# Strassen's scheme for two groups of each gate/up stage in a two-layer trunk

## The chip, the cores and the metric

The kernel runs on one core of one Trainium2 chip. The metric is the device time of one execution in microseconds (us); less is better.

## The reference

Two layers, each with a half-step SwiGLU, an attention mixer and a second half-step SwiGLU. There are 256 tokens, D_MODEL is 1024 and D_FF is 2816. The change lies in the four SwiGLUs, in the products with w_gate and w_up.

```python
def swiglu(h, w_gate, w_up, w_down):
    return (jax.nn.silu(h @ w_gate) * (h @ w_up)) @ w_down

for i in range(DEPTH):
    h = rmsnorm(x, ffn1_norm[i])
    x = x + 0.5 * swiglu(h, ffn1_w_gate[i], ffn1_w_up[i], ffn1_w_down[i])
    ...                       # projections, self and memory attention, w_out
    h = rmsnorm(x, ffn2_norm[i])
    x = x + 0.5 * swiglu(h, ffn2_w_gate[i], ffn2_w_up[i], ffn2_w_down[i])
```

## The kernel before

Every product of large matrices is made with three TensorE matmuls. Both operands are split into a rounded part (hi) and the rest (lo), and hi\*hi, hi\*lo and lo\*hi are summed in PSUM (`dense`, L409 to L426).

```python
nc.tensor.matmul(out=ps, lhsT=xh, rhs=wh, start=start, stop=False)
nc.tensor.matmul(out=ps, lhsT=xh, rhs=wl, start=False, stop=False)
nc.tensor.matmul(out=ps, lhsT=xl, rhs=wh, start=False, stop=stop)
```

Weights arrive in chunks of 128 x 2048 numbers (1 MB) in `raw` tiles, of which there are three (NRAW). ScalarE rounds a chunk into its `hi` tile, 512 columns at a time (`split_hi`, L321), and VectorE subtracts to get `lo` (`split_lo`, L340). There are four pairs of hi and lo tiles (NHL), called slots here; a slot is free again when the chunk's last matmul is through. So rounding can be up to four chunks ahead of TensorE.

A gate/up stage (`ffn`, L640 to L653) works through 11 groups of 256 gate and 256 up columns. A group needs two chunks (c = 0 and 1, the two halves of the 1024 rows) and both halves of the tokens (tb = 0 and 1). Each chunk is used by 8 calls of `dense`, which are 24 matmuls. `evac` (L517 to L562) takes a finished group out of PSUM: silu on ScalarE (L526), the product and a transpose on VectorE (L529, L537), a store to DRAM (`hd`, L543) and a load back (`hr`, L548), which turns it, then the split of `ht` (L557, L559).

The down stage that follows (L655 to L693) uses chunks of w_down. In three of the four SwiGLUs some chunks (SEVEN) are already done by a seven-product scheme: `split_lo` makes four differences of weights on VectorE (L334), `seven_forms` makes those of h, and `seven_sums` adds the products.

The input of a stage, `Xt`, is made by `prep_half` (L450 to L470): a transposed and scaled tile y, its rounded part xh and the rest xl. Small tiles of 128 x 512 numbers come from a pool of 19 (g2), larger ones from a pool of 12 (g4), and PSUM has 8 banks.

The order of all instructions is fixed while the program is built. `Flow` (L47 to L123) is a planner: it keeps a model clock (0.216 us a matmul, 0.07 + n/960 us on VectorE, 0.15 + n/1200 us on ScalarE, 2.9 us a chunk and 1.5 us latency for a load, 4.0 us from the issue of `hr` to its arrival), and generators add their instructions when the model says that what they wait for is there. Each engine then runs its own instructions in that order. All loads and stores stand in one queue, SP's. Work of `rope_setup` and of the memory's input (`memory_turn`) is mixed into the first stages.

Of the kernel before, what the change touches and what calls it, by code (L numbers as in the profile page):

```python
# [12 lines left out]
F32 = mybir.dt.float32  # L13
# [7 lines left out]
P = 128  # L21
# [121 lines left out]
def kernel(  # L143
# [96 lines left out]
    class Chunk:  # L240
        def __init__(self, parts):
            self.parts = parts
            self.raw = self.hi = self.lo = None
            self.arrive = self.early = None
            self.seven = False
            self.hit = [None] * 7
            self.lot = [None] * 7
            self.tt = [None] * 4
            self.uses = 0

        def part(self, lo, q):
# [13 lines left out]
    def add_chunk(parts, uses=8):  # L265
        c = Chunk(parts)
        c.uses = uses
        c.index = len(chunks)
        chunks.append(c)
        return c  # L270

    def loader():
        for i, c in enumerate(chunks):
# [3 lines left out]
            c.block = lambda q, c=c: c.raw[:, q * 512:(q + 1) * 512] if not c.seven else c.raw[:, (0, 2, 3)[q] * 512:  # L277
                                                                                          (1, 3, 4)[q] * 512]
# [26 lines left out]
    def split_hi():  # L305
        for i, c in enumerate(chunks):
            n = 2 if c.seven else 1
            yield lambda: c.raw is not None and hl_left[0] >= n
            hl_left[0] -= n
            yield c.early or c.arrive  # L310
            c.hi, c.lo = ([whl.tile([P, 2048], F32R, tag=x, name=f"{x}{i}_{j}") for j in range(n)] for x in ("hi", "lo"))
            if not c.seven:
                c.hi, c.lo = c.hi[0], c.lo[0]
            for q in range(7 if c.seven else 4):
                if q == 2:
                    yield c.arrive
                if c.seven and q >= 3:
                    yield lambda: c.tt[q - 3] is not None
                    yield c.tt[q - 3]
                yield calm_a(i)  # L320
                nc.scalar.copy(out=c.part(0, q), in_=c.block(q))  # L321
                c.hit[q] = flow.act(512)

    def split_lo():
        for i, c in enumerate(chunks):
            if c.seven:
                yield lambda: c.hi is not None and g2.left >= 6
                yield c.arrive
                r = [c.raw[:, q * 512:(q + 1) * 512] for q in range(4)]
                t = [g2.take([P, 512], F32, "wsum") for _ in range(4)]  # L330
                c.block = lambda q, r=r, t=t: ([r[0], r[2], r[3]] + t)[q]
                for j, x, y in ((0, r[1], r[0]), (1, r[3], t[0]), (2, r[3], r[1]), (3, r[2], t[1])):
                    yield calm_v(i)
                    nc.vector.tensor_sub(t[j], x, y)  # L334
                    c.tt[j] = flow.dve(512)
            for q in range(7 if c.seven else 4):
                yield lambda: c.hit[q] is not None
                yield c.hit[q]
                yield calm_v(i)
                nc.vector.tensor_sub(c.part(1, q), c.block(q), c.part(0, q).bitcast(F32))  # L340
                c.lot[q] = flow.dve(512)
                if q == 3:
                    raw_left[0] += 1
            if c.seven:
                g2.give(4)
# [16 lines left out]
    SEVEN = {(0, 1): (), (0, 2): (1, 4, 6), (1, 1): (1, 4, 6), (1, 2): (1, 4, 7)}  # L362

# [8 lines left out]

    def plan_ffn(l, nm, wg, wu, wd):
        gu = []
        for g in range(NG):
            ids = []
            for c in range(2):
                pieces = 2 if len(chunks) < 2 else 1
                a = cols4(wg[l], c, g * 256, 256, 0, pieces)
                b = cols4(wu[l], c, g * 256, 256, 256, pieces)  # L380
                ids.append(add_chunk([q for ab in zip(a, b) for q in ab]))
            gu.append(ids)
        plan[l, nm, "gu"] = gu
        dn = []
        for c in range(NG):
            dn.append(add_chunk(turned2(wd[l], c)))
            if c in SEVEN[l, nm]:
                dn[-1].seven, dn[-1].uses = True, 7
        plan[l, nm, "dn"] = dn
# [19 lines left out]
    def dense(ps, xh, xl, ready, c, need, sl, start, stop):  # L409
# [5 lines left out]
        wh, wl = (c.part(0, need), c.part(1, need)) if sl is None else (sl(c.hi), sl(c.lo))  # L415
# [8 lines left out]
        if c.uses == 0:  # L424
            hl_left[0] += 2 if c.seven else 1
# [14 lines left out]
    class Xt:  # L440
        def __init__(self):
# [6 lines left out]
            self.done = [0, 0]  # L448

    def prep_half(xt, tb, hf, gc, wait=0.0):  # L450
# [15 lines left out]
        g2.give()  # L466
# [44 lines left out]
    def ffn(l, nm, xt, gc_next):  # L511
# [5 lines left out]
        def evac(g, ps, end):  # L517
# [3 lines left out]
            for tb in range(2):  # L521
# [11 lines left out]
                banks.give()  # L533
# [15 lines left out]
            yield flow.now + 4.0  # L549
# [41 lines left out]
        def seven(c, ms):  # L591
# [3 lines left out]
            for q, j, m in ((0, 0, 0), (1, 1, None), (2, 6, None), (3, 3, 1), (4, 4, 2), (5, 5, 3), (6, 2, None)):  # L595
                ps = ms[m] if m is not None else acc.ps[q // 6][q // 2 % 2 if q < 6 else 0]
                t = dense(ps, ht[0][:, j], ht[1][:, j], lambda: htt[c], dn[c], q, None,
# [900 lines left out]
```

## Time and profile before

| | us |
|---|---|
| median of 3 runs (964.82 to 967.43) | 965.41 |
| the profiled execution, its own time | 964.95 |
| span of the profiled execution | 963.2 |
| TensorE busy | 954.8 |
| VectorE busy | 745.0 |
| ScalarE busy | 567.9 |

The gate/up stages lie at 9.0 to 130.6, 317.5 to 437.7, 496.9 to 617.1 and 781.2 to 901.4 us of the span; they are called stages 1 to 4 below. TensorE's granted clock is at its upper level from end to end. Busy time of TensorE is modelled and overlaps from one matmul to the next, so distances between starts say more than durations.

### The profile page before, as it was taken

The page shows a single profiled execution, that of the slowest core. Times are in us where ns is not written, and L with a number is a line of the kernel's source. Part 1 is how long each engine was busy: PE and PEld are TensorE (multiplying, and loading weights), DVE is VectorE, ACT ScalarE, POOL GpSimd, SP SyncE. Part 2 cuts the span into 40 slices and gives each one's busy share as a digit, 9 for nine tenths or more (in the row PEclk, how much of TensorE's full clock was granted, in tenths as well). Part 3 has the DMA queues.
Part 4 walks back from the last instruction along what each step waited for, and adds up shares of the span by engine and source line. Part 5 has one row for each costly group of instructions (what it writes and reads, how often), then busy time and mean ns, then how long its engine had stood idle before and what let it go on. Part 6 is the DMA issues. An engine that isn't in the chain of part 4 may idle for free.

```text
span 963.2 us, 13464 instructions
## 1 busy us (share of the span) xinstructions
PE 954.8 (99%) x4525; PEld 783.9 (81%) x4525; DVE 745.0 (77%) x1569; ACT 567.9 (59%) x1215; POOL 60.5 (6%) x65
## 2 busy tenths in 40 slices
PE   8999999999999999999999999999999999999998
PEld 7888888888777888888888888888787788888886
DVE  6777777788777877759986775797989886776785
ACT  6655555666676655545645555565677765554551
POOL 0000000021210000000000000000343100000000
PEclk9999999999999999999999999999999999999999
DMA  8988877486525479766568777666641468777661
GB/s 282 328 267 285 250 263 246 145 272 208 176 88 175 154 224 284 235 229 205 184 208 254 247 245 220 212 202 219 207 143 44 134 196 283 232 254 225 215 190 44
DMA packets 169295, 204.04 MB, mean 212 GB/s; under 512 B 9673, under 2 KB 144394, under 8 KB 169226
## 3 DMA queue, kind: packets, MB, share of 16 engines
q1 hardware_dynamic: 169226, 203.18, 66.0%
q8 instruction: 35, 0.57, 0.2%
q14 instruction: 34, 0.28, 0.1%
HBM read 188.99 MB, written 14.16 MB: 211 GB/s over the span
## 4 chain that ended last, share of the span: by engine, by line
PE 94%; DVE 3%; ACT 1%; DMA 1%; SPq 0%; issue 0%; ACTq 0%
PE gu L422 17%; PE gu L416 17%; PE gu L419 17%; PE acc L416 9%; PE acc L422 9%; PE acc L419 9%; PE pj L422 3%; PE pj L416 3%; PE pj L419 3%; PE xtp L429 1%; PE ptp L429 1%; PE S L1139 1%; PE AV L1220 1%; PE m L422 1%; PE m L419 1%; PE m L416 1%
## 5 line engine op out<-in xcount | busy, mean ns | idle before, releaser
L340 DVE TENSOR_TENSOR lo<-raw,hi 128x512 fp32r<-128x512 f32 x647 | 413.7, 684 | 103.9 <-ACT hi L321 100.0
L321 ACT CAST hi<-raw 128x512 fp32r<-128x512 f32 x647 | 361.7, 618 | 219.0 <-PE gu L422 123.6
L422 PE MATMUL gu<-hi,xl 128*128 128x512 f32 x704 | 274.3, 390 | 0.0
L416 PE MATMUL gu<-hi,xh 128*128 128x512 f32 x704 | 274.1, 389 | 0.0
L419 PE MATMUL gu<-lo,xh 128*128 128x512 f32 x704 | 274.0, 389 | 0.0
L422 PEld LDWEIGHTS gu<-hi,xl 128*128 128x128 f32 x704 | 132.2, 188 | 27.4
L419 PEld LDWEIGHTS gu<-lo,xh 128*128 128x128 f32 x704 | 132.2, 188 | 27.3
L416 PEld LDWEIGHTS gu<-hi,xh 128*128 128x128 f32 x704 | 132.2, 188 | 27.3
L416 PE MATMUL acc<-hi,ht 128*128 128x512 f32 x280 | 109.6, 391 | 0.0
L422 PE MATMUL acc<-hi,ht 128*128 128x512 f32 x280 | 109.2, 390 | 0.0
L419 PE MATMUL acc<-lo,ht 128*128 128x512 f32 x280 | 109.1, 390 | 0.0
L422 PE MATMUL pj<-hi,xl 128*128 128x512 f32 x160 | 64.5, 403 | 0.0
L419 PE MATMUL pj<-lo,xh 128*128 128x512 f32 x160 | 63.6, 397 | 0.0
L416 PE MATMUL pj<-hi,xh 128*128 128x512 f32 x160 | 63.5, 397 | 0.0
L422 PEld LDWEIGHTS acc<-hi,ht 128*128 128x128 f32 x280 | 52.6, 188 | 11.0
L419 PEld LDWEIGHTS acc<-lo,ht 128*128 128x128 f32 x280 | 52.6, 188 | 10.7
L416 PEld LDWEIGHTS acc<-hi,ht 128*128 128x128 f32 x280 | 52.6, 188 | 10.7
L526 ACT ACTIVATE sil<-gu,xr 128x256 f32<-128x256 f32 x88 | 41.5, 472 | 28.6 <-PE gu L422 28.6
L559 DVE TENSOR_TENSOR ht<-hr,ht 128x512 fp32r<-128x512 f32 x35 | 24.1, 687 | 32.2 <-ACT ht L557 32.2
L529 DVE SCALAR_TENSOR_TENSOR h<-gu,xr,sil 128x256 f32<-128x256 f32 x88 | 42.2, 479 | 5.8 <-ACT sil L526 4.5
L557 ACT CAST ht<-hr 128x512 fp32r<-128x512 f32 x35 | 21.6, 618 | 41.9 <-DMA hr<-hd 41.8
L436 POOL TENSOR_TENSOR xr<-v,nhalf 128x1 f32<-128x1 f32 x12 | 8.4, 698 | 502.3 <-DVE v L434 502.3
(191 smaller groups left out, 1069.0 us busy)
## 6 DMA issues: line engine op xcount, KB each, us to landing
raw<-in_ffn_w_down_dram SPq DMA_DIRECT2D x176, 256.0 KB, 4.1
raw<-in_ffn_w_gate_dram SPq DMA_DIRECT2D x86, 512.0 KB, 4.3
raw<-in_ffn_w_up_dram SPq DMA_DIRECT2D x86, 512.0 KB, 5.5
raw<-in_w_in_dram SPq DMA_DIRECT2D x32, 512.0 KB, 4.1
hd<-hb SPq DMA_DIRECT2D x44, 256.0 KB, 2.3
hr<-hd SPq DMA_DIRECT2D x44, 256.0 KB, 5.3
raw<-in_w_out_dram SPq DMA_DIRECT2D x8, 1024.0 KB, 5.0
raw<-in_w_mem_kv_dram SPq DMA_DIRECT2D x4, 1024.0 KB, 5.4
```

Of the source, the lines that this page charges most:

```text
L321: nc.scalar.copy(out=c.part(0, q), in_=c.block(q))
L340: nc.vector.tensor_sub(c.part(1, q), c.block(q), c.part(0, q).bitcast(F32))
L416: nc.tensor.matmul(out=ps, lhsT=xh, rhs=wh, start=start, stop=False)
L419: nc.tensor.matmul(out=ps, lhsT=xh, rhs=wl, start=False, stop=False)
L422: nc.tensor.matmul(out=ps, lhsT=xl, rhs=wh, start=False, stop=stop)
L429: nc.tensor.transpose(out=dst, in_=src, identity=flip if flipped else ident)
L526: nc.scalar.activation(sil, ps[tb][:, 0:256], AF.Silu, scale=xt.r[tb])
L529: nc.vector.scalar_tensor_tensor(out=h, in0=ps[tb][:, 256:512], scalar=xt.r[tb], in1=sil, op0=ALU.mult, op1=ALU.mult)
L557: nc.scalar.copy(out=hi, in_=src)
L559: nc.vector.tensor_sub(lo, src, hi.bitcast(F32))
L1139: nc.tensor.matmul(out=ss[e][:, pr, :nk], lhsT=q[rows, pr, :], rhs=k[rows, pr, :], start=i == 0, stop=i == len(passes) - 1)
L1220: nc.tensor.matmul(out=av[64 * e:64 * e + 64, pr, :], lhsT=vsrc(kb, pr, e), rhs=pts[e][:, pr, kb, :], start=(kb == 0), stop=(kb == nb - 1))
```

## The change

In each of the four gate/up stages two neighbouring groups are taken as a 2 x 2 block matrix times a 2 x 2 block matrix (tokens by rows, rows by groups) and are made with seven block products instead of eight. Groups 2 and 3 are taken in stage 1, and 3 and 4 in the others (PAIR). The four weight chunks r11, r12, r22 and r21 of the two groups give seven items b11, t1, t3, t2, b22, b21 and t4, each used by one block product of 12 matmuls (m1, m5, m7, m6, m3, m2, m4, in this order). t1 to t4 are differences of weights, four VectorE instructions each, before they are split. The items are mixed with the chunks of later groups (p): b11, p, t1, p, t3, p, t2, p, b22, p, p, b21, p, t4. `pair_forms` makes four combinations of y (four VectorE instructions) and splits them (four on each engine); y is kept for that. `pair_sums` copies m1 out of PSUM and adds the products with seven VectorE additions; `evac` then reads the sums from SBUF. A raw tile is held until the last item that reads it is split, and that of a SEVEN chunk until all seven splits are made, where before it was free after the fourth.

Plain chunks of gate/up (all but the first two of the kernel) and b11, b22, b21 are split 1024 columns at a time, t1 to t4 512. The planner takes 6.5 us instead of 4.0 for `hr`. The memory's transposes wait for VectorE a little less strictly, and `memory_prep` waits for all four memory tiles.

```diff
+    class Item:
+        def __init__(self, raws, uses=8, w=1):
...
+            self.n, self.frees, self.takes, self.gives = 1, 1, 0, 0
+            self.sums, self.t = [], []
+            self.index = len(items)
+            w = 1 if len(items) < 2 else w
+            self.units = [(self.own(q, w), q, w, None) for q in range(0, 4, w)]
...
     def split_hi():
+        for i, it in enumerate(items):
+            yield lambda: hl_left[0] >= it.n and all(r.raw is not None for r in it.raws)
...
+            for src, q, w, dep in it.units:
...
+                nc.scalar.copy(out=it.part(0, q, w), in_=src())
+                t = flow.act(512 * w)
...
     def split_lo():
+        for i, it in enumerate(items):
+            if it.sums:
+                yield lambda: all(r.raw is not None for r in it.raws) and g2.left >= it.takes + 2
+                yield max(r.arrive for r in it.raws)
+                it.t += [g2.take([P, 512], F32, "wsum") for _ in range(it.takes)]
+                for j, (x, y) in enumerate(it.sums):
                     yield calm_v(i)
+                    nc.vector.tensor_sub(it.t[j], x(), y())
+                    it.st[j] = flow.dve(512)
+            for src, q, w, dep in it.units:
...
+                nc.vector.tensor_sub(it.part(1, q, w), src(), it.part(0, q, w).bitcast(F32))
...
+            raw_left[0] += it.frees
+            g2.give(it.gives)
...
+    PAIR = {(0, 1): 2, (0, 2): 3, (1, 1): 3, (1, 2): 3}
...
+    def pair_items(raws):
...
+        def m1():
+            made["b11"] = plain(r11, 0)
+        def m5():
+            made["t1"] = sums([r12, r11], 0, 1)
+        def m7():
+            made["t3"] = sums([r22, r12], 0, 1)
+            made["t3"].gives = 4
+        def m6():
+            made["t2"] = sums([r22], 0, made["t1"], made["t1"])
+            made["t2"].frees = 0
+        def m3():
+            made["b22"] = plain(r22, 1)
+        def m2():
+            made["b21"] = plain(r21, 0)
+        def m4():
+            made["t4"] = sums([r21], 0, made["t2"], made["t2"])
+            made["t4"].gives = 4
...
+            for x in ("11", "m1", "p", "12", "m5", "p", "22", "m7", "p", "m6", "p", "m3", "p", "p", "21", "m2", "p", "m4"):
+                work.append(next(p) if x == "p" else x)
...
-            yield flow.now + 4.0
+            yield flow.now + 6.5
...
+        def pair_forms():
+            yield lambda: len(xt.y) == 4 and g4.left >= 4
...
+                yield lambda: flow.free["V"] <= flow.now + SLACK
+                op(y[o], y[a], y[b])
+                flow.dve(512)
+            for j, o in ((0, (1, 1)), (2, (1, 0)), (1, (0, 0)), (3, (0, 1))):
...
+                nc.scalar.copy(out=fm[j][:, 0], in_=y[o])
+                yield flow.act(512)
...
+                nc.vector.tensor_sub(fm[j][:, 1], y[o], fm[j].bitcast(F32)[:, 0])
...
+        def pair_sums():
...
+            nc.scalar.copy(out=u, in_=pb["m1"])
+            yield flow.act(512)
+            banks.give()
+            yield lambda: "m6" in mt and "m7" in mt
+            yield mt["m6"]
+            yield g2.has(3)
+            u2, w, v = (g2.take([P, 512], F32, "gu_v") for _ in range(3))
+            plus(u2, u, pb["m6"])
...
+            plus(w, u2, pb["m5"])
...
+            t = plus(v, w, pb["m7"])
...
+            plus(u2, u2, pb["m7"])
...
+            for m, (g, tb), x in (("m3", (1, 0), w), ("m2", (0, 0), u), ("m4", (0, 1), u2)):
...
+                t = plus(x, x, pb[m])
...
+        def product(m):
...
+            for k in range(4):
...
+                t = dense(pb[m], fh, fl, ready, pit[name], k, k == 0, k == 3)
...
-                yield lambda: flow.free["V"] <= flow.now
+                yield lambda: flow.free["V"] <= flow.now + SLACK
...
-        yield g2.has(8)
+        yield lambda: len(memd) == 4 and g2.left >= 8
```

## Rows read from the trace of the kernel before

**Rows 1.** Page, engines: busy us, share of the span, instructions.
```profile
PE 954.8 (99%) x4525; PEld 783.9 (81%) x4525; DVE 745.0 (77%) x1569; ACT 567.9 (59%) x1215; POOL 60.5 (6%) x65
```
**Rows 2.** Page, the chain that ended last: share of the span by engine.
```profile
PE 94%; DVE 3%; ACT 1%; DMA 1%; SPq 0%; issue 0%; ACTq 0%
```
**Rows 3.** Stretches: stages 1, 2 and 4, and the down stage after stage 3.
```profile
core 0: us, PE busy (x) PEld busy (x) DVE busy (x) ACT busy (x) POOL busy (x), PEclk, DMA share, GB/s
9.00:130.60 121.60, 121.33 (x540) 99.93 (x539) 93.47 (x183) 74.25 (x155) 2.59 (x4) 1.00 0.90 285
317.50:437.70 120.20, 120.20 (x534) 99.52 (x533) 89.48 (x205) 67.24 (x133) 1.81 (x2) 1.00 0.72 228
781.20:901.40 120.20, 120.20 (x534) 99.55 (x533) 85.38 (x164) 67.35 (x133) 1.50 (x2) 1.00 0.72 228
617.10:676.30 59.20, 59.20 (x268) 49.00 (x267) 50.92 (x89) 34.54 (x66) 0.55 (x1) 1.00 0.63 204
```
**Rows 4.** Timeline of PE (start, length, instruction), 78 matmuls in a row, ends shown.
```profile
39.75 0.39 PE L416 MATMUL gu<-hi,xh 128*128 128x512 f32 x1
...
57.20 0.39 PE L422 MATMUL gu<-hi,xl 128*128 128x512 f32 x1
```
**Rows 5.** Timeline of DVE: six in a row, and a difference that reads the one before.
```profile
48.18 3.76 DVE L340 TENSOR_TENSOR lo<-raw,hi 128x512 fp32r<-128x512 f32 x6
...
625.82 0.69 DVE L334 TENSOR_TENSOR wsum<-raw 128x512 f32<-128x512 f32 x1
626.54 0.69 DVE L334 TENSOR_TENSOR wsum<-raw,wsum 128x512 f32<-128x512 f32 x1
```
**Rows 6.** Groups by shape (busy us, mean ns): DVE subtractions of 512 and 256 columns.
```profile
L586 DVE TENSOR_TENSOR h<-sf,h 128x512 fp32r<-128x512 f32 x9 | 6.2, 686 | 0.3
...
L586 DVE TENSOR_TENSOR h<-hr,h 128x256 fp32r<-128x256 f32 x9 | 3.6, 395 | 0.0
```
**Rows 7.** Waits: who waited for whom: us in total, times, longest us.
```profile
ACT hi L321 <- PE gu L422: 123.6, 65, 2.9
DVE lo L340 <- ACT hi L321: 100.0, 85, 2.8
ACT ht L557 <- DMA hr<-hd: 41.8, 25, 2.8
```
**Rows 8.** Timelines of ACT and DVE in stage 2, a chunk split in full lead.
```profile
410.67 2.19 ACT L321 CAST hi<-raw 128x512 fp32r<-128x512 f32 x4 [2.85 <-PE gu L422]
...
411.32 2.50 DVE L340 TENSOR_TENSOR lo<-raw,hi 128x512 fp32r<-128x512 f32 x4 [2.18 <-ACT hi L321]
```
**Rows 9.** Timelines of DVE and PE, stage 4: fourth chunk's last lo, its first matmul.
```profile
790.61 4.29 DVE L340 TENSOR_TENSOR lo<-raw,hi 128x512 fp32r<-128x512 f32 x7
...
798.00 0.39 PE L416 MATMUL gu<-hi,xh 128*128 128x512 f32 x1
```
**Rows 10.** Timelines in stage 1: third chunk's last lo, its first matmul, waits for weights.
```profile
20.20 0.71 DVE L340 TENSOR_TENSOR lo<-raw,hi 128x512 fp32r<-128x512 f32 x1
...
21.39 0.39 PE L416 MATMUL gu<-hi,xh 128*128 128x512 f32 x1
...
24.85 2.18 ACT L321 CAST hi<-raw 128x512 fp32r<-128x512 f32 x4 [1.88 <-DMA raw<-in_ffn_w_up_dram]
...
38.63 2.18 ACT L321 CAST hi<-raw 128x512 fp32r<-128x512 f32 x4 [0.39 <-DMA raw<-in_ffn_w_up_dram]
```
**Rows 11.** Timeline of DVE, a down stage: idle before these two, none between them.
```profile
630.33 0.69 DVE L559 TENSOR_TENSOR ht<-hr,ht 128x512 fp32r<-128x512 f32 x1 [1.29 <-ACT ht L557]
...
649.24 2.50 DVE L340 TENSOR_TENSOR lo<-raw,hi 128x512 fp32r<-128x512 f32 x4 [0.73 <-ACT hi L321]
```
**Rows 12.** Page, DMA issues: count, KB each, median us to landing.
```profile
raw<-in_ffn_w_up_dram SPq DMA_DIRECT2D x86, 512.0 KB, 5.5
...
hr<-hd SPq DMA_DIRECT2D x44, 256.0 KB, 5.3
```

More of the change, by code (lines that the diff above doesn't have):

```diff
@@ L305, in split_hi @@
     def split_hi():
[L306 to L314, printed above, removed]
+        for i, it in enumerate(items):
+            yield lambda: hl_left[0] >= it.n and all(r.raw is not None for r in it.raws)
+            hl_left[0] -= it.n
+            yield max(r.early or r.arrive for r in it.raws)
+            it.hi, it.lo = ([whl.tile([P, 2048], F32R, tag=x, name=f"{x}{i}_{j}") for j in range(it.n)]
+                            for x in ("hi", "lo"))
+            for src, q, w, dep in it.units:
@@ L371, with seven_item @@
     WO = (0, 1, 2, 3)
-    def plan_ffn(l, nm, wg, wu, wd):
[L374 to L382, printed above, removed]
+    def seven_item(it):
+        r = [it.own(q) for q in range(4)]
+        t = lambda j: lambda: it.t[j]
+        it.n, it.uses, it.takes, it.gives = 2, 7, 4, 4
+        it.sums = [(r[1], r[0]), (r[3], t(0)), (r[3], r[1]), (r[2], t(1))]
+        it.units = [(r[0], 0, 1, None), (r[2], 1, 1, None), (r[3], 2, 1, None)] + [(t(j), 3 + j, 1, j) for j in range(4)]
@@ new lines, in pair_items, with sums, plain @@
+    def pair_items(raws):
+        r11, r12, r22, r21 = raws
+        def sums(need, x, y, held=None):
+            it = Item(need, 4)
+            it.t, it.takes = (held.t, 0) if held else ([], 4)
+            at_ = lambda v, j: it.own(j, 1, v) if isinstance(v, int) else (lambda: v.t[j])
+            it.sums = [(at_(x, j), at_(y, j)) for j in range(4)]
+            it.units = [((lambda j=j: it.t[j]), j, 1, j) for j in range(4)]
+            return it
+        def plain(r, frees):
+            it = Item([r], 4, 2)
+            it.frees = frees
+            return it
+        made = {}
+        def m1():
[15 more added lines that the diff above has]
+            made["t4"].gives = 4
+        return made, dict(m1=m1, m5=m5, m7=m7, m6=m6, m3=m3, m2=m2, m4=m4)
@@ L383, in plan_ffn @@
         plan[l, nm, "gu"] = gu
+        plan[l, nm, "work"] = [w for w in work if w not in ("11", "12", "22", "21")]
+        if pair is not None:
+            plan[l, nm, "pair"] = made
         dn = []
@@ L515, in ffn, with evac @@
         prog = [-1]
-        def evac(g, ps, end):
+        def evac(g, ps, end, gives=None):
             hb = None
@@ L654, in ffn @@
+        if pair is not None:
+            flow.spawn(pair_forms())
+        work = list(plan[l, nm, "work"])
+        if (l, nm) != (0, 1):
+            for tb in range(2):
+                for c in range(2):
+                    plain_chunk(0, c, (tb,))
+            work = work[2:]
+        for w in work:
+            if isinstance(w, str):
+                product(w)
+            else:
+                plain_chunk(*w, range(2))
         flow.until(banks.has(4))
         acc = Acc()
-        nxt = None if gc_next is None else Xt()
+        nxt = None if gc_next is None else Xt(nm == 2 and PAIR[l + 1, 1] is not None)
```

198 lines of the change are left out of this document (128 added, 70 removed).

## The prediction

> **What bounds the kernel now.** I read the page's engine table first: TensorE is busy 99% of the span [rows 1], and the chain that ended last is 94% TensorE [rows 2]. Since its busy time is modelled, I then looked at starts. In stage 1 the first matmul of a run of 78 starts at 39.75 us and the last at 57.20 [rows 4], so 17.45 / 77 = 0.2266 us a matmul, with no hole. A stage has 528 of these, 119.7 us, and the stretches of stages 2 and 4 are 120.2 us long [rows 3], a few transposes included: the gate/up stages are bound by TensorE's stream from end to end. Every matmul taken out is worth 0.2266 us, as long as weights stay split ahead of it. So the second thing to read is how far ahead they are, and how much VectorE, which must do most of the new work, has left.
>
> The waits show it. ScalarE's roundings wait most for TensorE's last use of a slot (123.6 us), and VectorE's subtractions for those roundings (100.0 us) [rows 7]: both sit idle because all four slots are full. In stage 2 ScalarE is let go at 410.67, and VectorE has the chunk split at 411.32 + 2.50 = 413.82 [rows 8]. TensorE has just begun the first of the three chunks in front, 3 x 24 x 0.2266 = 16.3 us of work. The full lead is thus 410.5 + 16.3 - 413.8 = 13.0 us. VectorE is busy 85.4 us of stage 4, 89.5 of stage 2, and 93.5 of stage 1 [rows 3].
>
> **The change part by part.** *Matmuls.* Eight block products become seven, 96 matmuls become 84, in four stages: 48 x 0.2266 = 10.9 us off TensorE's stream. Shapes stay, so I expect the same distance. The Trainium skill (TensorE: Matmul & The Clock Gate, section on the back-to-back issue gap) gives about 216 ns for 512 columns; by that the 48 would be worth an estimated 10.4 us. The row shows 0.2266, and the row decides.
>
> *VectorE.* Six subtractions in a row take 3.76 us, the single one 0.686 [rows 5, 6]: a distance of (3.76 - 0.69) / 5 = 0.615 us. Per stage there are new: 16 differences of weights, 12 more splits (28 quarters for 16), 8 instructions for the combinations of y, 7 additions; 43 x 0.615 = 26.4 us. The wide split saves little. A 1024-column subtraction isn't in the trace; from 256 to 512 columns it grows by 0.686 - 0.395 = 0.291 us [rows 6], so I take 0.615 + 2 x 0.291 = 1.197 for 1.230, 0.03 saved, 42 times, 1.4 us (bounds: nothing, and the 0.615 of one whole instruction each). VectorE then has 85.4 + 26.4 - 1.4 = 110.4 us in a stage of 120.2 - 2.7 = 117.5, and 118.5 of 118.9 in stage 1. It fits, barely, so the order in time matters.
>
> *The lead in stages 2 to 4.* I follow it item by item: lead of the next = lead + TensorE's time for this item - VectorE's time for the next. TensorE: 5.44 for a plain chunk, 2.72 for a block product. VectorE: 85.4 / 22 = 3.9 for a plain chunk with all that belongs to it, 8 x 0.615 = 4.9 for t1 to t4, 2.5 for b11, b22, b21. The lowest start is stage 4, where the fourth chunk's last lo ends at 790.61 + 0.69 and is wanted at 798.00 [rows 9]: 6.7 us. The combinations of y fall just there: 6.7 - 4.9 = 1.8. Two plain chunks give back 1.5 each, b11 3.0: 7.8 at b11. Then p 6.6, t1 7.1, p 6.0, t3 6.5, p 5.3, t2 5.8, p 4.6, and four sums fall due (2.5): b22 5.1, p 3.9, and with one group's `evac` (4 x 1.4 us for two groups, so 2.8) and a sum p 2.0, b21 5.0, p 3.8, t4 3.7, p 2.5, and after the last evac about 0.7. From there it grows by 1.5 a chunk. It stays above nothing; I add 0.4 us for the three stages together, with 0 and 2 as bounds. VectorE can hold such a pace: in the down stage after stage 3 it works without a gap from 630.33 to its wait before 649.24, 18 us, [rows 11] with nothing lost on TensorE there.
>
> *Loads.* r11, r12 and r22 are held while they are shared, and three raw tiles are all there are. r22 can only be loaded when t1 is split. A load takes 5.5 us at the median [rows 12], then come four differences, one rounding and four subtractions, some 11.2 us from t1 to t3, where TensorE takes 2.72 + 5.44 = 8.2. That costs 3 us of lead once and caps t3 at 7.1 - 3.0 = 4.1, about 2.4 below the row above; VectorE makes this wait good with other work, so I keep the sum and count it in the bounds. In SP's queue that load waits ahead of `hd` and `hr`, which the down stage needs only after the remaining chunks, five of them at the least (27 us).
>
> *Stage 1.* Here the lead isn't there yet. The third chunk's last lo ends at 20.20 + 0.71 = 20.91 and its chunk is wanted at 21.39; ScalarE still waits for weights at 24.85 and at 38.63 [rows 10]. The last quarter is used 3 x 0.68 = 2.0 us after the first, so the slack is 2.5 us; the combinations of y take 4.9 about then: 2.4 us stall, unless they fall into a wait for weights. Later the shared items take some 7 us of lead (7.8 to 0.7 above) from the 3 to 5 there can be by then: 2 to 4 more. Stage 1 pays between 0 and 7 us; I take 3.5.
>
> *At nothing.* The later rounding of h ends waits of ScalarE for `hr` (41.8 us, 25 times [rows 7]; 5.3 us to land [rows 12] where the planner took 4.0). No matmul waited behind them, so it gains nothing now, but it keeps ScalarE free where the lead is thin; an `hr` tile is held 2.5 us longer. ScalarE gets some 17 instructions more, and has 67 of 120 us [rows 3]. In the down stages a raw tile of a SEVEN chunk comes free three subtractions, 1.8 us, later; three raws in turn and the lead hide that. The memory's input may come later, since it wants nine free small tiles while the new items hold up to eight; its products stand behind the first down stage, whose 61 us I count as its cover.
>
> **The sum.** -10.9 + 3.5 + 0.4 = -7.0 us of the span of 963.2 us: 956.2, with the 1.75 us around it 957.95 for the profiled execution, which lay 0.46 under the median. On the median: 965.41 - 7.0 = 958.4.
>
> **The rivals.** *The cover holds everywhere.* No stall in stage 1 either: 965.4 - 10.9 = 954.5. For it: VectorE has little queued behind the startup's loads, and the sum was made with leads to the last quarter. Against: stage 1's weights still land late at 38 us.
>
> *Stage 1 pays in full, the others 0.5 to 1 each.* 965.4 - 10.9 + 7 + 1.5 to 3 = 963.0 to 964.5. For it: 118.5 of 118.9 us there.
>
> *VectorE can't hold 0.615 (slower).* The leads above end 0.7 us above nothing after some 105 subtraction-lengths (64 us / 0.615). Each 0.01 us more per instruction takes 1.05 us of lead per stage: the stall begins at 0.622, and at 0.65 the three stages lose 3 x 3.0 us, which with stage 1 is all of the gain; that is the point from which it decides. At the full 0.686 they lose 3 x 6.8 = 20 us: 965.4 - 10.9 + 3.5 + 20 = 978. For it: a difference that reads the one before it starts 0.72 us after it [rows 5], and the additions of `pair_sums` are such a chain. Against: these are few, and plain runs hold 0.615. The Trainium skill speaks for this rival (VectorE: DVE Perf Modes, "The DRAIN you can't avoid"): an instruction doesn't start until the pipeline has emptied, which would make the duration the cost. The trace disagrees for a run of subtractions, 0.615 apart where one lasts 0.686.
>
> *It doesn't do what it says*: fewer matmuls, but further apart, by the many short accumulations: 84 instead of 96 only pays below 0.2266 x 96 / 84 = 0.259 us. No row speaks for it.
>
> **How the numbers follow.** A measurement here can tell about 0.3%, 2.9 us, from no change, so faster means below 962.5. Forecast (956 to 961) 0.45; cover everywhere (954 to 956) 0.25; stage 1 in full (961 to 965) 0.20, of which 0.12 below 962.5; slower by VectorE's pace 0.07; the last 0.03, near no change. Faster 0.82, the same 0.11, slower 0.07. The range runs from 954.0 to 963.5: it takes in the cover, and most of the third case, and leaves out less than 2 in 10.
>
> **What would show it.** 4477 matmuls instead of 4525, 0.2266 us apart in m1 to m7. Stages 2 to 4 117.2 to 118.5 us long, stage 1 121 to 125. Holes between starts in stage 1 at the second to fourth chunk and from m7 on, put down to lo (L340's successor), and few elsewhere. ScalarE's wait for slots well under 123.6 us, VectorE near 90% in these stages. The forecast is wrong if holes stand before m7, m6 or m4 in stages 2 to 4, or if the wide splits take far from 1.2 us of VectorE, or if the memory's products come late at the end of the first down stage.

## The result, and the profile after

The changed kernel takes 968.37 us (median of 13 runs, 967.03 to 971.44), the kernel before 965.28 beside it (13 runs): ratio 1.0029, interval 1.0017 to 1.0041. I had forecast 958.4. The times of either kernel differ by up to 5 us from run to run; the profiled execution of after took 970.04 with a span of 968.2, so the accounts below, made of spans, start from 968.2 - 963.2 = +5.0 us, where the medians are 3.1 apart.

First the page of after (engines: busy, share, instructions; then the chain that ended last), which answers [rows 1, 2]:

```profile
PE 951.2 (98%) x4477; PEld 775.1 (80%) x4477; DVE 828.5 (86%) x1577; ACT 586.3 (61%) x1119; POOL 61.9 (6%) x65
...
PE 65%; DVE 17%; DMA 11%; ACT 3%; issue 2%; SPq 1%; POOL 0%; DVEq 0%; ACTq 0%; POOLq 0%
```

The 48 matmuls are gone, but the chain, 94% TensorE before, is 65% TensorE now and runs through VectorE (17%) and DMA (11%). Something that was covered is not covered any more. The table by stretch says where: stages 1 to 4, and fifth the down stage after stage 3, against [rows 3].

```profile
core 0: us, PE busy (x) PEld busy (x) DVE busy (x) ACT busy (x) POOL busy (x), PEclk, DMA share, GB/s
9.00:140.60 131.60, 125.44 (x529) 99.00 (x528) 109.88 (x176) 76.59 (x129) 3.86 (x4) 0.97 0.78 251
328.40:446.00 117.60, 117.60 (x522) 97.43 (x521) 106.93 (x175) 72.02 (x110) 2.54 (x2) 1.00 0.73 230
505.20:622.70 117.50, 117.50 (x522) 97.34 (x521) 105.91 (x173) 70.65 (x108) 0.86 (x1) 1.00 0.75 240
788.50:906.40 117.90, 117.87 (x522) 97.30 (x521) 106.15 (x167) 71.21 (x111) 1.50 (x2) 1.00 0.72 229
622.70:683.60 60.90, 59.70 (x268) 48.75 (x268) 53.12 (x102) 35.61 (x70) 0.55 (x1) 1.00 0.62 203
```

Counted from the first matmul of a stage to the first of the next one, stages 2, 3 and 4 are 2.7, 2.7 and 2.4 us shorter, about what 12 matmuls each were to give. Stage 1 ends 10.05 us later than before, at 140.66 instead of 130.61. The down stage after stage 3 is 1.8 us longer, the first mixer 1.1. Sum: 10.05 + 1.8 + 1.1 - 7.9 = +5.0. So the question is stage 1: it takes 131.5 us where 12 matmuls fewer should leave 121.6 - 2.7 = 118.9. It lost 12.6 us.

Part of that is the clock. Timeline of PE in stage 1, holes (the bracket is the idle time and what ended it; a hole is counted below as the distance between two starts less the usual 0.227 us, a little more than the bracket), and under it stretches of after: one ahead of the holes, and two that follow some of them.

```profile
44.41 0.51 PE L496 MATMUL gu<-hi,xh 128*128 128x512 f32 x1 [0.81 <-ACT hi L326]
45.67 0.51 PE L499 MATMUL gu<-lo,xh 128*128 128x512 f32 x1 [0.76 <-DVE lo L344]
...
69.91 0.50 PE L499 MATMUL gu<-lo,xh 128*128 128x512 f32 x1 [2.12 <-DVE lo L344]
```
```profile
39.70:43.20 3.50, 3.50 (x17) 2.89 (x16) 0.92 (x2) 0.11 (x1) 0.00 (x0) 1.00 0.79 277
46.70:50.10 3.40, 3.40 (x9) 2.66 (x8) 0.50 (x2) 0.00 (x0) 0.00 (x0) 0.50 0.86 270
70.80:73.70 2.90, 2.90 (x8) 2.31 (x7) 2.90 (x4) 0.00 (x0) 0.00 (x0) 0.50 0.91 256
```

After the holes at 43.2 and 44.4 us, and again after the one at 67.4, TensorE ran at its lower level, 1.2 GHz (0.50), for about 3 us: the same matmuls start 0.427 us apart there instead of 0.227, so seven or so cost 1.4 us more each time. The eight longest holes are 7.3 us together, the two slow stretches 2.8. The clock alone doesn't make after the slower kernel: two of its 13 runs have a mean granted clock of 1.000, and they took 967.36 and 968.37 us.

What did stage 1 wait for? The waits of SyncE (SP in the rows), which issues the loads, from 9 to 130 us (us in total, times, longest), first in the kernel before, then after:

```profile
SPq L281 <- DVE lo L340: 21.2, 17, 3.5
SPq L548 <- DMA hd<-hb: 3.0, 3, 1.7
```
```profile
SPq L288 <- DVE lo L344: 32.7, 13, 4.2
SPq L632 <- DMA hd<-hb: 20.0, 6, 5.1
```

The second line has grown from 3.0 to 20.0 us. Timelines of SP and of DVE about the first holes show what it does (start, length, instruction):

```profile
38.35 0.42 SPq L627 DMA_DIRECT2D hd<-hb  x1
43.92 0.37 SPq L632 DMA_DIRECT2D hr<-hd  x1
44.38 0.62 SPq L288 DMA_DIRECT2D raw<-in_ffn_w_gate_dram  x1
45.05 0.46 SPq L288 DMA_DIRECT2D raw<-in_ffn_w_up_dram  x1
45.56 0.46 SPq L288 DMA_DIRECT2D raw<-in_ffn_w_gate_dram  x1
```
```profile
44.39 2.36 DVE L344 TENSOR_TENSOR lo<-raw,hi 128x1024 fp32r<-128x1024 f32 x2 [3.77 <-ACT hi L326]
...
49.65 2.69 DVE L338 TENSOR_TENSOR wsum<-raw,raw 128x512 f32<-128x512 f32 x4 [2.90 <-DMA raw<-in_ffn_w_up_dram]
```

`hr` reads from DRAM what `hd` writes there, so SyncE stands at `hr` until `hd` has landed, 5.5 us. The weight loads stand behind it, though VectorE has nothing to do (idle 3.77 and 2.90 us in these rows). The kernel before had the same two DMAs, but mostly with a weight load between them, issued while `hd` was under way:

```profile
38.50 0.34 SPq L543 DMA_DIRECT2D hd<-hb  x1
39.67 0.37 SPq L281 DMA_DIRECT2D raw<-in_ffn_w_gate_dram  x1
...
42.12 0.37 SPq L548 DMA_DIRECT2D hr<-hd  x1
```

In after no load stands between the first three such pairs. It seemed to me that the raw tiles held for the pair of groups leave none to put there; that wasn't shown, and run e10 (below) speaks against it.

### The profile page after: what moved, and what is told of

Its sections match the earlier page's. It is cut to its first block, busy times and chain, and to the rows that moved or that the text cites. A ratio compares the mean times of both kernels' runs of the same rounds, so it can differ in the third digit from the quotient of the medians.

```text
span 968.2 us, 13306 instructions
## 1 busy us (share of the span) xinstructions
PE 951.2 (98%) x4477; PEld 775.1 (80%) x4477; DVE 828.5 (86%) x1577; ACT 586.3 (61%) x1119; POOL 61.9 (6%) x65
## 4 chain that ended last, share of the span: by engine, by line
PE 65%; DVE 17%; DMA 11%; ACT 3%; issue 2%; SPq 1%; POOL 0%; DVEq 0%; ACTq 0%; POOLq 0%
PE gu L499 9%; PE gu L502 9%; PE gu L496 8%; PE acc L496 7%; DVE lo L344 7%; PE acc L499 7%; PE acc L502 7%; DMA raw<-in_ffn_w_up_dram 4%; PE pj L502 2%; DMA hd<-hb 2%; ACT hi L326 2%; PE pj L499 2%; PE pj L496 2%; DVE wsum L338 2%; DMA raw<-in_ffn_w_down_dram 2%
## 5 line engine op out<-in xcount | busy, mean ns | idle before, releaser
L326 ACT CAST hi<-raw 128x512 fp32r<-128x512 f32 (+1 forms) x467 | 335.5, 769 | 160.0 <-DMA raw<-in_ffn_w_up_dram 53.1
L344 DVE TENSOR_TENSOR lo<-raw,hi 128x512 fp32r<-128x512 f32 (+1 forms) x467 | 390.3, 871 | 31.6 <-ACT hi L326 31.3
L499 PE MATMUL gu<-lo,xh 128*128 128x512 f32 x576 | 226.5, 393 | 4.3 <-DVE lo L344 4.1
L496 PE MATMUL gu<-hi,xh 128*128 128x512 f32 x576 | 226.0, 392 | 0.8 <-ACT hi L326 0.8
L502 PE MATMUL gu<-hi,xl 128*128 128x512 f32 x576 | 225.8, 392 | 0.0
L499 PEld LDWEIGHTS gu<-lo,xh 128*128 128x128 f32 x576 | 108.9, 189 | 30.3 <-DVE lo L344 7.8
L496 PEld LDWEIGHTS gu<-hi,xh 128*128 128x128 f32 x576 | 109.0, 189 | 24.1 <-ACT hi L326 1.2
L502 PEld LDWEIGHTS gu<-hi,xl 128*128 128x128 f32 x576 | 108.9, 189 | 22.3
L326 ACT CAST hi<-wsum 128x512 fp32r<-128x512 f32 x100 | 58.5, 619 | 24.3 <-DVE wsum L338 21.5
L344 DVE TENSOR_TENSOR lo<-wsum,hi 128x512 fp32r<-128x512 f32 x100 | 63.1, 682 | 0.0
L641 ACT CAST ht<-hr 128x512 fp32r<-128x512 f32 x35 | 21.6, 618 | 49.3 <-DMA hr<-hd 49.3
```

What stands on the lines that cost most here:

```text
L326: nc.scalar.copy(out=it.part(0, q, w), in_=src())
L344: nc.vector.tensor_sub(it.part(1, q, w), src(), it.part(0, q, w).bitcast(F32))
L641: nc.scalar.copy(out=hi, in_=src)
```

## The experiments

My theory when I began them: stage 1's loss is `hr` on SyncE's queue. The rivals: three raw tiles are too few while the pair holds them; VectorE can't keep up from a cold start; the memory's transfers crowd the weights. Stage 1 is taken from its first matmul to the first of the down stage, in the profiled execution; "pair" is the first of the two groups in stage 1. Such a length is of one execution: the first matmul comes at 8.8 to 11.6 us, and in e2, e4, e7, e11 and e12 the stage begins with 2 to 5 us at the lower clock, so a difference of a microsecond or two between two lengths says little. The medians are of all runs.

| run | pair | `hd`, `hr` on | raw tiles | median us | ratio (95%) | stage 1 us |
|---|---|---|---|---|---|---|
| before | none | SyncE | 3 | 965.3 | | 121.6 |
| after | 2 | SyncE | 3 | 968.37 | 1.0029 (1.0017 to 1.0041) | 131.5 |
| e1 | none | SyncE | 3 | 960.36 | 0.9946 (0.9930 to 0.9963) | 121.7 |
| e5 | 2 | GpSimd | 3 | 961.64 | 0.9963 (0.9949 to 0.9977) | 125.8 |
| e2 | 4 | SyncE | 3 | 962.21 | 0.9969 (0.9959 to 0.9979) | 126.8 |
| e10 | 2 | SyncE | 4 | 970.60 | 1.0053 (1.0033 to 1.0074) | 130.7 |
| e11 | 2 | GpSimd | 4 | 967.28 | 1.0016 (1.0005 to 1.0027) | 125.4 |
| e12 | 4 | GpSimd | 4 | 962.73 | 0.9976 (0.9966 to 0.9986) | 120.8 |
| e13 | 2, no differences | GpSimd | 4 | 961.98 | 0.9966 (0.9954 to 0.9978) | 119.0 |
| e9 | none | GpSimd | 3 | 958.19 | 0.9928 (0.9908 to 0.9948) | 121.3 |
| e14 | 4 | GpSimd | 3 | 958.66 | 0.9937 (0.9918 to 0.9957) | 120.3 |
| e15 | 4 | GpSimd | 4 | 955.58 | 0.9900 (0.9883 to 0.9916) | 119.3 |

**Is it stage 1?** One run without its pair.

```diff
-    PAIR = {(0, 1): 2, (0, 2): 3, (1, 1): 3, (1, 2): 3}
+    PAIR = {(0, 1): None, (0, 2): 3, (1, 1): 3, (1, 2): 3}
```

> Stage 1 without its pair (all 528 matmuls), stages 2 to 4 as in the changed kernel. If stage 1 is all of the loss and the others keep their 2.7 us each: stage 1 back at 121.4 to 122 us, total 957 to 959 us. If the wide split or the later h are what hurts stage 1, it stays above 125 us and the total above 962.

960.36 us, 8.0 less than after, with stage 1 at 121.7 us as before. SyncE's wait for `hd` up to 130 us is 7.8 us here instead of 20.0, so most of it comes with the pair. The scheme is worth its price where a lead exists; in stage 1 alone it cost all that the others saved and more.

**Is it the queue?** `hd` and `hr` go to GpSimd's queue; the other engines keep their order of instructions to the last one.

```diff
-            nc.sync.dma_start(out=hd.rearrange("a i b x -> (a i) (b x)"), in_=hb.rearrange("p b t f j -> p (b t f j)"))
+            nc.gpsimd.dma_start(out=hd.rearrange("a i b x -> (a i) (b x)"), in_=hb.rearrange("p b t f j -> p (b t f j)"))
...
-            nc.sync.dma_start(out=hr, in_=hd.rearrange("a i b x -> (i b) a x"))
+            nc.gpsimd.dma_start(out=hr, in_=hd.rearrange("a i b x -> (i b) a x"))
```

> Store and load of h issued from GpSimd's queue instead of SP's; the instructions of TensorE, VectorE and ScalarE are the same in the same order. SP's queue theory: weights are loaded as soon as a raw tile is free, stage 1 falls from 131.5 to 122 to 126 us, total 959 to 963. Cold start or VectorE's load: stage 1 stays within 2 us of 131.5 us, total 966 to 970.

Stage 1 falls from 131.5 to 125.8 us; about 2.8 us of the difference are the two slow stretches, which e5, at the upper clock all through stage 1, doesn't have. The timeline of SP for the same stretch of the same program:

```profile
36.95 0.37 SPq L288 DMA_DIRECT2D raw<-in_ffn_w_gate_dram  x1
37.36 0.50 SPq L288 DMA_DIRECT2D raw<-in_ffn_w_up_dram  x1
37.90 0.48 SPq L288 DMA_DIRECT2D raw<-in_ffn_w_gate_dram  x1
38.43 0.50 SPq L288 DMA_DIRECT2D raw<-in_ffn_w_up_dram  x1
```

These two chunks are asked for at 36.95 and 37.90; in after they are the ones of 44.38 and 45.56. This run also settles the two small losses elsewhere: the down stage after stage 3 is back at 59.25 us and from the last matmul of the first down stage to stage 2 it takes 125.9 us, as before. In that down stage after had shown the same picture, four weight loads, `hd`, and 4.6 us later `hr` ahead of the next loads, and some 30 us on TensorE waiting for lo:

```profile
629.16 2.53 SPq L288 DMA_DIRECT2D raw<-in_ffn_w_down_dram  x4
631.73 0.58 SPq L627 DMA_DIRECT2D hd<-hb  x1
636.37 0.36 SPq L632 DMA_DIRECT2D hr<-hd  x1
636.84 22.30 SPq L288 DMA_DIRECT2D raw<-in_ffn_w_down_dram  x20
```
```profile
669.48 0.50 PE L499 MATMUL acc<-lo,ht 128*128 128x512 f32 x1 [0.84 <-DVE lo L344]
```

So of the spans' difference the queue is 968.2 - 959.7 = 8.5 us: 5.7 in stage 1, 1.8 in that down stage, and 1.1 in the first mixer. On the medians it is 6.7.

The same wait can also be shortened by issuing `hr` later, when `hd` is nearer to its end:

```diff
             g2.give()
+            yield flow.now + 4.0
             yield g2.has()
             hr = g2.take([P, 4, P], F32, "hr")
```

> The planner puts the load of hr 7 us after its store instead of 3, so the store has landed and SP doesn't stand still before the weights behind it. SP's queue theory: SP's wait for hd in stage 1 falls from 21.0 us to under 5, stage 1 from 131.5 us to 123 to 127, total 960 to 964. Cold start alone: stage 1 stays within 2 us of 131.5, total 966 to 970.

962.87 us (ratio 0.9973, 0.9963 to 0.9983). SyncE's wait for `hd` from 9 to 140 us falls from 21.0 to 3.1, that for VectorE's lo rises to 51.7, and stage 1 is still 128.3 us long, 1.3 more than I had expected at most. It takes the wait of the queue away and leaves the rest, which I still had to find.

**Is it the memory's transfers?** They go to GpSimd's queue too.

```diff
-        nc.sync.dma_start(out=d.rearrange("a i b x -> (a i) (b x)"), in_=src.rearrange("p b t k j -> p (b t k j)"))
+        nc.gpsimd.dma_start(out=d.rearrange("a i b x -> (a i) (b x)"), in_=src.rearrange("p b t k j -> p (b t k j)"))
...
-        nc.sync.dma_start(out=r.rearrange("p a t k j -> p a (t k j)"), in_=d.rearrange("a i b x -> (i b) a x"))
+        nc.gpsimd.dma_start(out=r.rearrange("p a t k j -> p a (t k j)"), in_=d.rearrange("a i b x -> (i b) a x"))
...
-            nc.sync.dma_start(out=m, in_=mem[0, :, q * 256:(q + 1) * 256].rearrange("(b p) d -> p b d", p=P))
+            nc.gpsimd.dma_start(out=m, in_=mem[0, :, q * 256:(q + 1) * 256].rearrange("(b p) d -> p b d", p=P))
```

> As e5_h_on_pool, and the memory's loads and stores from GpSimd's queue too, so SP issues nothing but weights, gains and x. With h alone moved, stage 1 was 125.8 us and SP still stood 10.2 us before the memory's store. SP's queue theory: stage 1 falls to 120 to 123 us, total 957 to 960. VectorE's load in stage 1, or the raw tiles held at a cold start: stage 1 stays at 125 us or more, total 961 or more.

963.36 us (0.9976, 0.9964 to 0.9989), no better than e5; stage 1 is 124.9 us, and the mixer behind it 1.8 longer. I had expected 120 to 123: the memory isn't the cause.

**Is it the place?** The pair two groups later, when there has been more time to build a lead; on SyncE's queue, and then with the edits of e6.

```diff
-    PAIR = {(0, 1): 2, (0, 2): 3, (1, 1): 3, (1, 2): 3}
+    PAIR = {(0, 1): 4, (0, 2): 3, (1, 1): 3, (1, 2): 3}
```

> Stage 1's pair on groups 4 and 5 instead of 2 and 3, after eight plain chunks instead of four. Cold start (the pair comes before the lead is built): stage 1 falls to 119 to 121 us, total 955 to 957. VectorE's total in stage 1 too high (118 of 119 us), wherever the pair stands: stage 1 stays at 125 us or more, total 961 or more. SP's queue (the load of h waits for its store, weights behind it): in between, since a lead of 12 us covers one such wait.

962.21 us, stage 1 126.8. Now there is one hole, of 4.4 us at 114.8, and its cause stands in SP's timeline:

```profile
108.68 0.45 SPq L627 DMA_DIRECT2D hd<-hb  x1
116.34 0.36 SPq L632 DMA_DIRECT2D hr<-hd  x1
116.76 0.50 SPq L288 DMA_DIRECT2D raw<-in_ffn_w_gate_dram  x1
```

It is the queue again, 7.1 us of waiting for `hd`. What the later place saves, 4.7 us, should then be the other cause.

> Stage 1's pair on groups 4 and 5, and h and the memory on GpSimd's queue; TensorE, VectorE and ScalarE run the same instructions in the same order as in e2_first_at_4, where stage 1 took 126.8 us with one hole of 4.4 us. SP's queue theory: stage 1 at 119 to 121 us, total 954 to 957, the 10.9 us of the 48 matmuls in full. VectorE's load (118 of 119 us) as the cause: stage 1 stays at 124 us or more, total 960 or more.

960.70 us (0.9943, 0.9923 to 0.9963), and 127.6 us for stage 1: by what I had written, both speak for VectorE's load and against the queue. The profile is of its slowest run, 967.26, where stage 1 begins with some 5 us at the lower clock and has a hole of 2.2 us, for lo, at 117.9, so the length says little; but the best runs, 957.8 to 958.6, lie above the 954 to 957 that I had expected too. The expectation failed, and the run leaves open why; e14 below is the same without the memory's transfers.

**What do the other parts of the change do?** All gate/up weights split 512 columns at a time; and h rounded as early as before.

```diff
-            it = Item([r], 4, 2)
+            it = Item([r], 4, 1)
...
-                gu[w] = add_chunk(parts(*w), 8, 2)
+                gu[w] = add_chunk(parts(*w), 8, 1)
```

> All weights of gate/up split 512 columns at a time again, everything else as in the changed kernel. If the wide split helps by its saving (42 times 0.03 to 0.08 us a stage), VectorE has 1.5 to 3.5 us more in each stage, and stage 1 gets up to 4 us longer: total 968 to 973. If it hurts, because the first quarter comes later where the lead is thin: 963 to 967.

973.04 us (1.0067, 1.0048 to 1.0085). Stages 2 to 4 are as short as in after (117.4 each), but stage 1 is 137.4 us. So the wide split, which I had put at 1.4 us of VectorE's time, is worth 5.9 us there (4.7 on the medians) and nothing where a lead is. That points to the work of splitting in stage 1; VectorE's part and ScalarE's, whose roundings get cheaper too (last section), aren't told apart by this run.

```diff
-            yield flow.now + 6.5
+            yield flow.now + 4.0
```

> The planner takes 4.0 us for hr again, everything else as in the changed kernel. The plan is another one after that, so a few us either way say little. If the later rounding costs nothing and gains nothing: within 2 us of 968.4. If the earlier rounding lets ScalarE stand before h while weights wait: ScalarE's wait for hr in stage 1 goes from 6 to over 10 us, total 970 to 974. If the later rounding is itself the harm, 962 to 965.

975.14 us (1.0095, 1.0077 to 1.0114), stage 1 135.3 us, and the down stage after stage 2 is 2.9 longer. ScalarE's wait for `hr` is 94.0 us over the kernel instead of 49.3. I had put the later rounding down at nothing; with leads this thin it is worth 6.8 us, with the other plan that comes with it.

**Is it the number of raw tiles?** A fourth one, paid for with two of the twelve large slots; on SyncE's queue (e10), with the edit of e5 (e11), and with the pair at 4 too (e12).

```diff
-    NRAW, NHL, NT2 = 3, 4, 19
+    NRAW, NHL, NT2 = 4, 4, 19
...
-    gp = ctx.enter_context(tc.tile_pool(name="gp", bufs=12))
+    gp = ctx.enter_context(tc.tile_pool(name="gp", bufs=10))
...
-    g4 = Slots(flow, gp, "g", 12)
+    g4 = Slots(flow, gp, "g", 10)
```

> A fourth raw tile, paid for with two of the twelve four-KB slots; the pair stays at groups 2 and 3 and hd and hr stay on SyncE. Theory (the part of stage 1's loss that GpSimd's queue did not cure, about 6 us, is that three raw tiles are held by the pair, so that weights wait for VectorE's release): stage 1 falls from 131.5 to 124 to 127, and SyncE's wait for lo in it falls well under 33 us. Rival A (only the wait of hr matters, and it delays the fourth tile's load as well): 130 to 132. Rival B (VectorE's own work in stage 1 is the bound): 130 to 132 with VectorE busy without gaps where the holes are. Fewer four-KB slots may cost the down stages 0 to 3 us.

> A fourth raw tile, and hd and hr on GpSimd's queue. Theory (queue and raw tiles are the two causes): stage 1 is 119 to 121.5 us, which is the 119 that seven products in place of eight leave and at most 2.5 of the start, and the time is 955 to 958. Rival (something else, VectorE's pace or the memory, holds stage 1): it stays at 124 to 126, as it was with the queue alone changed (125.8).

Stage 1 is 130.7 us (after: 131.5) and 125.4 (e5: 125.8). My theory of the held raw tiles falls: at this place a fourth tile gives next to nothing on either queue. Nor does it fill the gap between `hd` and `hr`; SyncE's wait for `hd` in e10 is longer than the 20.0 us of after:

```profile
SPq L632 <- DMA hd<-hb: 26.4, 8, 5.0
```

The totals are worse than without it, since the memory's products after the first down stage take 6 to 7 us more (in e11 28.6 for 22.0). But e11 shows what it is instead. Stretches 20 to 60 and 60 to 100 us (columns as above):

```profile
20.00:60.00 40.00, 39.81 (x176) 32.40 (x175) 39.90 (x64) 26.72 (x41) 5.48 (x8) 1.00 0.84 261
60.00:100.00 40.00, 36.80 (x157) 28.57 (x156) 35.19 (x57) 23.96 (x43) 4.41 (x7) 1.00 0.72 232
```

VectorE is busy 39.90 of the 40 us up to 60: it waits for nothing, weights included, and gains no lead. TensorE's large holes come after it, from 72 on, the longest (2.1 us) at 91.8, where VectorE stood 2.04 us at the subtraction for `ht`, with t4's four splits behind it:

```profile
90.31 0.45 DVE L621 STREAM_TRANSPOSE hb<-h 128x256 f32<-128x256 f32 x1
92.80 0.69 DVE L643 TENSOR_TENSOR ht<-hr,ht 128x512 fp32r<-128x512 f32 x1 [2.04 <-ACT ht L641]
93.41 2.49 DVE L344 TENSOR_TENSOR lo<-wsum,hi 128x512 fp32r<-128x512 f32 x4
```

With a lead such a wait is covered; without one it is a hole.

> As the run with four raw tiles and hd and hr on GpSimd's queue, with the pair of stage 1 at groups 4 and 5. Theory (queue and raw tiles are the causes; the place matters little once they are gone): stage 1 119 to 121 us, within 1.5 us of the run with the pair at 2, time 954 to 957.5. Rival (the start is the cause: the place decides): over 2 us shorter than with the pair at 2.

Stage 1 is 120.8 us, 4.6 less than e11 (as the medians are), which differs in the place alone: the expectation's rival, that the place decides.

**Is it VectorE's work?** e11 once more, with the sixteen differences of stage 1 left out (the plan is still empty only there); the blocks are split as they are, so what stage 1 computes for these groups isn't the product. With them go the small tiles that held them, and the wait of a split for its difference.

```diff
             it = Item(need, 4)
             it.t, it.takes = (held.t, 0) if held else ([], 4)
             at_ = lambda v, j: it.own(j, 1, v) if isinstance(v, int) else (lambda: v.t[j])
+            if not plan:
+                it.takes = 0
+                it.units = [(it.own(j), j, 1, None) for j in range(4)]
+                return it
...
-            made["t3"].gives = 4
+            made["t3"].gives = 4 if plan else 0
...
-            made["t4"].gives = 4
+            made["t4"].gives = 4 if plan else 0
```

> The run with four raw tiles and hd and hr on GpSimd's queue, pair at groups 2 and 3; in stage 1 the sixteen differences of weights (t1 to t4) are left out, and the blocks are split as they are, so that what stage 1 computes there is not the product; 16 x 0.615 = 9.8 us of VectorE's work are gone and nothing else of the loads, the matmuls or the queues. Theory (what holds stage 1 once the queue is mended is VectorE, which had no idle time from 20 to 61 us and so built up no lead before the pair's work came): stage 1 falls from 125.4 to 119.5 to 122, and the holes at 91 to 99 us go. Rival (weights or the wait for hr on VectorE's queue hold it): 124 or more.

```profile
20.00:60.00 40.00, 39.81 (x176) 32.51 (x175) 35.30 (x51) 28.22 (x46) 5.24 (x8) 1.00 0.95 301
60.00:100.00 40.00, 40.00 (x178) 32.83 (x177) 35.68 (x58) 25.87 (x43) 4.47 (x7) 1.00 0.86 275
```

Stage 1 is 119.0 us, its holes of over half a microsecond are gone, and VectorE is busy 35.30 of the 40 us. 9.8 us of VectorE's work gave back 6.4 us of stage 1, and 5.3 on the medians. The second cause is the work itself, at a time when there is no lead to pay for it.

**Putting it together.** No pair in stage 1, `hd` and `hr` on GpSimd's queue (e1's and e5's edits); the pair at 4 and the queue (e2's and e5's); and the same with a fourth raw tile, this time for four of the nineteen small tiles.

> No pair in stage 1, and hd and hr on GpSimd's queue. Theory: both causes of the loss are gone; stage 1 is like the one of before, 121 to 122 us, stages 2 to 4 stay at 117.2 to 117.7, the holes in the down stages are absent, and the time is 955 to 958. Rival (the late issue on GpSimd costs elsewhere, as it made ht late before): the time is 959 to 962, no better than the run without the first pair alone (960.4).

> Three raw tiles, hd and hr on GpSimd's queue, pair of stage 1 at groups 4 and 5. Theory (queue and place are two causes that add up: the queue was worth 5.7 us at place 2, the place 4.7 on either queue): stage 1 is 126.8 - 5.7 = 121 (120 to 122) us, time 955 to 958. Rival (the fourth raw tile is what mended it at place 4): stage 1 124 or more, time 959 to 962.

```diff
-    NRAW, NHL, NT2 = 3, 4, 19
+    NRAW, NHL, NT2 = 4, 4, 15
```

> As that, with a fourth raw tile that is paid for with four of the nineteen small tiles, while the four-KB slots stay at twelve. Theory: stage 1 120 to 122 as with ten four-KB slots (120.8), and the memory's products after the first down stage take 22 us again where they took 28 with ten slots; time 954 to 958. Rival (it is the small tiles that run short): holes in the mixer or in stage 1, time 960 or more.

e9: 958.19 us, stage 1 121.3, no hole in it or in the down stages, just above the 955 to 958 that I had expected. e14: 958.66, just above its range too, stage 1 120.3, so the fourth tile is not what mends it. e15: 955.58 us, 0.9900 of before (0.9883 to 0.9916), the best of all. Its memory products take 22.0 us, so it was the large slots that they lacked in e10 to e12. Its four stages (the 14 us of POOL are mostly the issuing of `hd` and `hr`, which now lies there):

```profile
9.10:128.40 119.30, 119.09 (x528) 97.40 (x526) 111.11 (x175) 77.72 (x128) 14.36 (x21) 1.00 0.87 276
315.90:433.30 117.40, 117.40 (x521) 97.23 (x520) 106.09 (x173) 71.37 (x110) 15.46 (x22) 1.00 0.72 233
492.60:610.00 117.40, 117.40 (x521) 97.21 (x520) 109.27 (x177) 70.69 (x108) 14.06 (x21) 1.00 0.77 246
773.70:891.80 118.10, 117.74 (x521) 97.19 (x521) 105.28 (x166) 71.34 (x111) 14.60 (x22) 1.00 0.71 231
```

Against [rows 3], and by first matmuls for stage 3, they are shorter by 2.3, 2.8, 2.7 and 2.1 us. VectorE does 111.11 us of work in stage 1, more than in after, and TensorE hardly waits for it: its total was not too much, only when it fell due.

Do the two causes add up? From the 131.5 us of stage 1 the queue takes 5.7 (e5) and the place 4.7 (e2); both together 11.2 (e14), where the sum is 10.4. But e14's profile is of its fastest run, and after's and e2's are slower than their medians. On medians the queue is worth 6.7 us at place 2 and 3.6 at place 4, the place 6.2 and 3.0: together 9.7 of 12.9, so the two overlap by some 3 us. What stays open: e14's runs lie between 956.3 and 962.2 and e15's within 0.1 us, though their profiles differ by 0.8; that the fourth tile steadies the leads is likely and wasn't shown.

## Why the prediction was wrong, point by point

- *TensorE's stream, 48 x 0.2266.* Right: 4477 matmuls; 33 distances from 35.73 to 43.21 us are 0.2267 on average; stages 2 to 4 are 2.7, 2.7 and 2.4 us shorter. The rival of matmuls further apart is out.
- *The lead in stages 2 to 4*, 0.4 us (0 to 2). Right: no hole there in after. VectorE has 106 to 107 us in a stage, where I had 110.4. The wide split is most of the difference: I had taken 1.197 us for 1024 columns, and in a row they are 1.12 apart (rows in the last section), against 2 x 0.615 = 1.23: 0.11 x 42 = 4.6 saved for 1.4.
- *VectorE can't hold 0.615.* Out: no stall in stages 2 to 4, and 1024-column subtractions that last 1.22 us start 1.12 apart (last section). The rule of the Trainium skill that spoke for this rival (VectorE: DVE Perf Modes, "The DRAIN you can't avoid"), by which an instruction starts only when the pipeline has emptied, again doesn't set the pace of a run of subtractions here; the same section adds that an instruction that is not held starts earlier. These rows, 1.12 apart where one lasts 1.22, agree with that.
- *Loads.* **The step that failed.** I wrote that in SP's queue the load of r22 waits ahead of `hd` and `hr`, which are needed much later, and looked no further. I saw who is harmed when h waits behind weights and not who is harmed when weights wait behind h. `hr` can't be issued until `hd` has landed. [rows 12] has landing times for loads; the one that mattered, that of `hd`, I didn't ask for, and its median of 2.3 us in the kernel before (the page's list of DMA issues) would have been too low: in after `hr` followed 5.6 us behind `hd`. The kernel before had only 3.0 us of this wait, with a weight load standing between the two; with the pair in the plan it is 20.0. Why the plan then puts no load there stays open. The price, 5.7 us in stage 1 (2.8 of them by way of the clock) and 2.9 elsewhere, was no term of the sum.
- *Stage 1*, 3.5 us with bounds of 0 and 7. The mechanism was right, the size was not: with the queue mended, stage 1 still loses 125.8 - 118.9 = 6.9 us, the upper bound. I had added up 2.4 at the start and 2 to 4 later and then taken the middle. The lead that I granted for the pair, "3 to 5", had no row of its own; VectorE almost without idle time from 20 to 60 us (39.90 of 40 in e11) shows that it gained none there. The 118.5 us of VectorE's work in 118.9 were a warning that I had in the text; measured it is 109.9, and it was still too much, since an average over a stage says nothing of its first half.
- *At nothing.* The raw tile of a SEVEN chunk that comes free later, and the memory's input: right, with `hd` and `hr` out of the way (e5) nothing is lost in the down stages or the mixer. The later rounding of h: wrong in a way that helped, 6.8 us (e8). The clock wasn't in the sum at all: after some holes TensorE ran at its lower level, 2.8 us in the profiled execution.
- *The range.* Its upper end was the rival in which stage 1 pays in full, 963 to 964.5; e5 (961.64 us) is about that case. The 968.37 of after needed a second cause on top of it. I had given a slower kernel 0.07, all of it for VectorE's pace, and nothing for the queue. The prediction's sum with both terms as measured is 963.2 - 10.9 + 6.9 + 5.7 + 2.9 = 967.8 for the span of 968.2.
- *Signs.* I had put the holes of stage 1 at its second to fourth chunk and from m7 on; none of the eight longest is at the early chunks, and they begin right behind m5, the second block product, at 43 us, in the wait for weights. ScalarE's wait for slots fell from 123.6 to 30.8 us, as forecast, and its wait for weights (53.1 us) took its place, which I hadn't looked for.

## What to carry to other kernels

Before work is added to an engine with room, find the stretch where its lead is smallest and add up there, not over the stage: the same work was free in three stages and cost 6 to 7 us in the one that starts cold. For each DMA that waits for another one, ask what stands behind it in its queue, and whether the new order still has a load to fill the gap; moving a store and the load that reads it back to another queue than the weights gave 6.7 us here, while moving the memory's transfers as well gave nothing. And a place that is hurt by a change can often be moved or left out: three quarters of this change, or all of it with stage 1's pair two groups later and h on a queue of its own, beat both kernels, by 0.5 to 1% of the one before.

## What the runs showed of the hardware that I had not expected

- The clock can fall behind short holes: two of 1.0 us each, at 43.2 and 44.4 us, were followed by about 3 us at the lower level, and one of 2.3 us at 67.4 again, each time 1.4 us on top. It needn't: in e5 a hole of 2.5 us at 61.2, and in e11 one of 2.1 us at 91.8, left TensorE at its upper level. The stretch of e5 (columns as above):

```profile
60.00:70.00 10.00, 7.63 (x34) 5.98 (x33) 7.81 (x9) 3.22 (x4) 0.00 (x0) 1.00 0.58 186
```

- A 1024-column subtraction on VectorE takes 1.22 us, and four in a row start (4.59 - 1.22) / 3 = 1.12 apart, against 0.686 and 0.615 for 512; a rounding on ScalarE takes 1.048 against 0.618. Timeline of DVE in after, then groups by shape (busy us, mean ns, idle before):

```profile
24.84 1.22 DVE L344 TENSOR_TENSOR lo<-raw,hi 128x1024 fp32r<-128x1024 f32 x1
...
27.33 4.59 DVE L344 TENSOR_TENSOR lo<-raw,hi 128x1024 fp32r<-128x1024 f32 x4
```
```profile
L344 DVE TENSOR_TENSOR lo<-raw,hi 128x1024 fp32r<-128x1024 f32 x164 | 195.9, 1214 | 17.7 <-ACT hi L326 17.6
...
L326 ACT CAST hi<-raw 128x512 fp32r<-128x512 f32 x303 | 169.4, 618 | 59.9 <-DMA raw<-in_ffn_w_down_dram 21.0 <-issue 11.8 <-PE acc L502 9.0
L326 ACT CAST hi<-raw 128x1024 fp32r<-128x1024 f32 x164 | 166.1, 1048 | 100.1 <-DMA raw<-in_ffn_w_up_dram 52.1 <-PE gu L502 28.1 <-issue 9.7
```

- From the issue of `hd`, 256 KB to DRAM, to that of the load that reads it went 5.6 us in stage 1 of after (38.35 to 43.92) and 7.7 in e2 (108.68 to 116.34), where the page of before has a median of 2.3 us for `hd` to land.
